# Regrouping the recurrent step of a bidirectional RWKV-7 layer by TensorE tile size

## The chip, the cores and the metric

The kernel runs on one core of one Trainium2 chip, as one program. The metric is the device time of one execution in microseconds (us). Before the change the median of three runs is 1908.73 us (1905.5 to 1909.22).

## The reference

Two layers work on 1024 latent tokens and 256 context tokens of width 1024, in float32. The first layer holds 12 RWKV-7 heads of width 64 and a Fourier mixing; the second is a multi-scale retention. What concerns us is the state recurrence of the first layer, which runs in both directions (`d == 1` reversed), context before latents:

```python
def step(s, inp):
    r_t, w_t, k_t, v_t, kk_t, b_t = inp
    sa = jnp.einsum('bhij,bhj->bhi', s, kk_t)
    s = s * w_t[:, :, None, :] - sa[..., None] * b_t[:, :, None, :] + v_t[..., None] * k_t[:, :, None, :]
    return s, jnp.einsum('bhij,bhj->bhi', s, r_t)
```

The outputs of both directions are added, each head is normalised over its 64 values, multiplied by a gate, and projected.

## The kernel before, in words

**The chunks.** The recurrence is computed in chunks of 64 tokens: 1280 tokens make 20 chunks. A *step* handles one chunk of four heads (two head pairs `q`) in both directions `d`; the index `x` = 2`d`+`q` and the half `h` name the eight units of a step. Three groups of four heads make 60 steps, `s` = 0 to 59; `c` is the chunk within its group. Inside a chunk the sequential dependence becomes a triangular 64x64 system for each unit. Its matrix comes out of the *scores* (product of the chunk's keys `bkp` with its queries `arr`, then a mask), and the step multiplies by the inverse of it.

**The inverse.** It is made in 32x32 blocks. GpSimd inverts the two diagonal blocks of all units of eight steps at once: 8 steps x 8 units x 2 blocks are its 128 partitions. `inv` does this in 31 rows, each a multiply (L1183) and an add (L1185) on a tile `z` with the triangle `tl`. The triangles reach it through DRAM: `diag` (L1142) writes the scores of each step to `dn`, and `fetch_tl` (L1170) reads `tl` back. The result goes to DRAM as `dz` (L1189), and `bring` (L1201) spreads it, in four transfers for four steps, over a tile `zs`. The off-diagonal block is made on TensorE in two small products, `offd1` (L1218, whose right side `x1p` VectorE transposes at L1206) and `offd2` (L1229).

**The step.** On TensorE a step issues: `ws` (L1423), scores of a later step (L1135), `up` (L1451), `offd1` of the next step, four transposes `pt` (`tok`, L1161), the state's increment `pst` into `ws` (L1488), `offd2`, the part of the output that comes from the state (L1513), the part from this chunk (L1516), and the other direction's scores (L1135). ScalarE copies `ws` to `wt` (L1428, two copies) and `up` to `vu` (L1456). VectorE adds state and increment into a tile `tmp` (L1492), multiplies by the decay `pc` into `vu` (L1496) and into the next state (L1497), and masks the scores (L1138).

**What sets the order.** The order is that of the program text, engine by engine; each engine and each DMA queue runs its own list in order. Scores run `L` = `LL` steps ahead of the step. The 31 rows of an inversion are dealt out over four *slots* of each step (`RW`), and `rows_until(s)` issues the rest, and `bring`, when step `s` needs them. `norm` is the head normalisation of 256 tokens, a generator that `stage` advances once in a step: TensorE centres (`pcen`, L1243), VectorE reduces (`rv`, L1252 and L1253), GpSimd takes the power -1/2 and multiplies (L1254 and L1258, the *pair* in what follows), TensorE transposes (`pgn`, L1262). All transfers named here but `dz` are issued by SyncE (SP), whose list they share with the loads of `arr`, `bkp` and `vu`.

Of the kernel before, what the change touches and what calls it, by code (L numbers as in the profile page):

```python
# [1039 lines left out]
def phaseB(g):  # L1040
# [83 lines left out]
    def scores(s, ds=(0, 1)):  # L1124

        if not 0 <= s < NS:
            return
        if s % 8 == 0 and ds[0] == 0:
            DN[s // 8] = dr.tile([steps(s // 8), 8, 64, 64], F32, tag="dn", name=f"dn{s // 8}")
        sc = SC[s] = SCR[s % (L + 1)]  # L1130
        ps = ps2.tile([128, 2, 512], F32, tag="psc", name=f"psc{s}_{ds[0]}")
        for d in ds:
            for x in (2 * d, 2 * d + 1):
                for h in range(2):
                    mm(ps[:, h, 128 * x : 128 * x + 128], lhsT=BK[s][H[h], x, :], rhs=AR[s][H[h], x, :], start=True, stop=True, tile_position=(64 * h, 0))  # L1135
# [1072 lines left out]
```

## Time and profile before

| | us |
|---|---|
| median of three runs | 1908.73 |
| profiled execution | 1913.79 |
| its span | 1912.0 |
| projections and gates, to 657.50 | 657.50 |
| start of the recurrence, to 695.52 | 38.02 |
| 60 steps, 695.52 to 1166.85 | 471.33 |
| second layer and projections, to the end | 745.15 |

The numbers of the next sections come from the one profiled execution, whose times count from the start of its span. In the 60 steps TensorE is busy for 389.50 us, GpSimd for 284.96, ScalarE for 259.61 and VectorE for 253.94, at a granted TensorE clock of 0.91 of full speed. Before them the share is 580.32 of 657.50 us for TensorE, and behind them 723.65 of 745.15 us. A line's row gives its start, its duration, the engine, the line, out<-in, the tile's form, and in brackets how long the engine was idle ahead of it and what ended that. A group of matrix products is shown as one row; its duration includes a modelled end, so the distance between two starts is the better measure of a group.

### The profile page before, as it was taken

How to read it: one execution, taken by the hardware profiler on the slowest of the kernel's cores; microseconds unless marked ns; L12 is line 12 of the kernel's file. 1: busy time of each engine (PE TensorE's matmuls, PEld its weight loads, DVE VectorE, ACT ScalarE, POOL GpSimd, SP SyncE). 2: the span in 40 equal slices, each digit the busy share in tenths (PEclk: the TensorE clock that was granted, in tenths of full speed). 3: DMA queues.
4: the chain of work that ended last, by engine and by line, in shares of the span. 5: the costliest groups of instructions: out<-in, count | busy, mean ns of one | idle time of the engine just before them, and what ended most of it. 6: DMA issues, size and time to landing. Idle time of an engine off the chain costs nothing. (4 is left out here: it accounts for less than half of the span.)

```text
span 1912.0 us, 37942 instructions
## 1 busy us (share of the span) xinstructions
PE 1708.9 (89%) x15490; PEld 1438.3 (75%) x15490; DVE 1009.5 (53%) x1580; ACT 715.4 (37%) x1598; POOL 773.9 (40%) x894
## 2 busy tenths in 40 slices
PE   6999997879887766887888788999999999999998
PEld 4777776667765655776777676779889898898877
DVE  6532689888985144655565444553352533523643
ACT  5322544535431123555556565343221122212231
POOL 4331443343452717656686821122442414414310
PEclk9999999899998978998899888999999999999999
DMA  9571365446559365777777774442111101101162
GB/s 316 172 239 55 86 169 146 136 122 187 136 147 279 104 163 154 202 194 181 191 191 192 193 201 129 134 139 87 39 50 34 56 23 46 58 30 56 50 204 99
DMA packets 340529, 257.54 MB, mean 135 GB/s; under 512 B 109004, under 2 KB 291780, under 8 KB 340100
## 3 DMA queue, kind: packets, MB, share of 16 engines
q1 hardware_dynamic: 325796, 221.96, 41.7%
q10 hardware_dynamic: 10512, 18.62, 3.3%
q0 software_dynamic: 4048, 14.55, 2.1%
q8 instruction: 122, 2.00, 0.4%
q14 instruction: 51, 0.42, 0.1%
HBM read 175.20 MB, written 79.88 MB: 133 GB/s over the span
## 5 line engine op out<-in xcount | busy, mean ns | idle before, releaser
L1183 POOL TENSOR_TENSOR tp<-z,tl 128x31 f32<-128x31 f32 (+19 forms) x248 | 130.8, 527 | 135.2 <-DMA tl<-dn 116.9
L548 PE MATMUL pgm<-hh,wh 128*128 128x512 f32 (+1 forms) x624 | 170.4, 383 | 0.0
L548 PE MATMUL pgm<-hl,wh 128*128 128x512 f32 (+1 forms) x624 | 160.9, 367 | 0.0
L548 PE MATMUL pgm<-hh,wl 128*128 128x512 f32 (+1 forms) x624 | 159.6, 365 | 0.0
L526 POOL TENSOR_TENSOR wl<-wr,wh 128x512 fp32r<-128x512 f32 x60 | 86.6, 1447 | 179.6 <-ACT wh L524 179.6
L1185 POOL TENSOR_TENSOR z<-z,tp 128x31 f32<-128x31 f32 (+19 forms) x248 | 139.7, 563 | 19.4
L1135 PE MATMUL psc<-arr,bkp 64*128 64x128 f32 x960 | 87.0, 312 | 52.9 <-issue 23.3
L548 PEld LDWEIGHTS pgm<-hl,wh 128*128 128x128 f32 x624 | 107.2, 196 | 20.5 <-POOL hl L484 1.0
L548 PEld LDWEIGHTS pgm<-hh,wl 128*128 128x128 f32 x624 | 106.6, 194 | 19.3
L548 PEld LDWEIGHTS pgm<-hh,wh 128*128 128x128 f32 x624 | 104.3, 197 | 20.8 <-issue 6.2
L1135 PEld LDWEIGHTS psc<-arr,bkp 64*128 64x128 f32 x960 | 67.7, 204 | 66.0 <-issue 36.9
L1862 PE MATMUL pv<-wv,hh 128*128 128x256 f32 x640 | 117.2, 285 | 0.0
L1138 DVE TENSOR_TENSOR scr<-psc,mask 128x512 f32<-128x512 f32 x120 | 80.4, 687 | 61.3 <-PE psc L1135 61.3
L571 DVE SCALAR_TENSOR_TENSOR m<-pgm,dv,m 128x255 f32<-128x255 f32 (+2 forms) x108 | 105.1, 987 | 10.5 <-ACT m L561 7.7
L1492 DVE TENSOR_TENSOR tmp<-ws,state 128x256 f32<-128x256 f32 x54 | 22.9, 424 | 152.6 <-PE ws L1488 75.2
L1862 PEld LDWEIGHTS pv<-wv,hh 128*128 128x128 f32 x640 | 99.6, 192 | 0.1
L1601 PE MATMUL pow_eo<-w_eo,yhw_eo 128*128 128x512 f32 x320 | 90.2, 403 | 0.5 <-ACT w_eo L1567 0.4
L1862 PE MATMUL pv<-wv,hl 128*128 128x256 f32 x320 | 90.6, 283 | 0.0
L1428 ACT COPY wt<-ws 64x256 f32<-64x256 f32 x120 | 43.9, 366 | 88.9 <-PE ws L1423 87.4
L835 POOL TENSOR_TENSOR ar<-m,Pp 128x640 f32<-128x640 f32 (+2 forms) x30 | 36.5, 1226 | 98.6 <-ACT Pp L827 93.9
L1601 PE MATMUL pow_oo<-w_oo,yhw_oo 128*128 128x512 f32 x256 | 72.3, 397 | 0.5 <-DVE w_oo L1568 0.4
L1601 PEld LDWEIGHTS pow_eo<-w_eo,yhw_eo 128*128 128x128 f32 x320 | 60.7, 191 | 16.0 <-ACT w_eo L1567 1.1
(337 smaller groups left out, 4179.7 us busy)
## 6 DMA issues: line engine op xcount, KB each, us to landing
aw<-ada_w SPq DMA_DIRECT2D x16, 1024.0 KB, 10.1
wr<-w_ev SPq DMA_DIRECT2D x60, 256.0 KB, 3.8
scr_AR<-ar SPq DMA_DIRECT2D x24, 640.0 KB, 3.7
scr_BK<-bk SPq DMA_DIRECT2D x24, 640.0 KB, 4.8
arr<-scr_AR SPq DMA_DIRECT2D x60, 256.0 KB, 3.7
bkp<-scr_BK SPq DMA_DIRECT2D x60, 256.0 KB, 4.3
br<-scr_BK ACTq DMA_DIRECT2D x60, 256.0 KB, 4.3
x<-xin SPq DMA_DIRECT2D x20, 512.0 KB, 4.9
```

The lines of the kernel that those rows point to most:

```text
L526: nc.gpsimd.tensor_tensor(out=wl, in0=wr, in1=wh.bitcast(F32), op=ALU.subtract)
L548: g.nc.tensor.matmul(ps[:, b, :n], lhsT=st[:, k % 4, :], rhs=mv[:, k, c0 : c0 + n], start=(k == 0 and i == 0), stop=(k == 7 and i == 2))
L571: nc.vector.scalar_tensor_tensor(out=o, in0=i, scalar=g.muc[:, q, ft : ft + 1], in1=o, op0=ALU.mult, op1=ALU.add)
L835: nc.gpsimd.tensor_tensor(out=ar[:, cs, 64:128], in0=ch(proc(self.r, d, lo, n)), in1=Pp[:, cs, 1:65], op=ALU.mult)
L1135: mm(ps[:, h, 128 * x : 128 * x + 128], lhsT=BK[s][H[h], x, :], rhs=AR[s][H[h], x, :], start=True, stop=True, tile_position=(64 * h, 0))
L1138: tt(out=sc[:, 2 * d : 2 * d + 2], in0=src, in1=K["mask2"][:, d].unsqueeze(1).unsqueeze(1).broadcast_to([128, 2, 2, 128]), op=ALU.mult)
L1183: eng.tensor_tensor(out=tv, in0=ZZ[:, 0:k, s : s + 1].broadcast_to([U, k, n]), in1=TL[:, s : s + 1, s + 1 : 32].broadcast_to([U, k, n]), o ...
L1185: eng.tensor_tensor(out=zo, in0=zo, in1=tv, op=ALU.add)
L1428: nc.scalar.copy(WT2[H[h], h].rearrange("p x v -> p (x v)"), WS[H[h], 0:256])
L1492: tt(out=tmp, in0=inc, in1=STS[s % 2], op=ALU.add)
L1601: self.g.nc.tensor.matmul(ps[:, 512 * b : 512 * b + 512], lhsT=st[:, k, :], rhs=mv[:, 512 * b : 512 * b + 512], start=(k == 0 and i == 0), ...
L1862: mm(ps[:, 256 * e : 256 * e + 256], lhsT=st[:, k, c0 : c0 + 128], rhs=mv[:, k, :], start=(k == 0 and i == 0), stop=(k == 7 and i == 2))
```

## The change

- The TensorE work of a step is put in another order, by the size of the tile that a product uses. `scores` now computes both directions of one step at once, as 16 products on 64x64 tiles. `offd1`, the state's part of the output, `up` and the scores stand in a row; then `pst`, the chunk's part of the output and `offd2`; then `tok`.
- `up` works on 64x64 tiles with one `wt` of 128x256, written by one ScalarE copy (L1431) in place of two.
- `offd1` no longer reads `x1p`. GpSimd makes the transposed upper diagonal blocks itself: after an inversion it copies half of `z`, transposed, into the buffer `tl` (L1179), and writes that to DRAM as `dx` (L1180). `bring` adds four transfers for four steps (L1189), which put the transposed blocks into the score tiles `scr`. The two VectorE transposes of a step go.
- The sum of increment and state stays in PSUM (L1462), so that the multiplications by `pc` (L1464, L1465) read PSUM.
- Scores run 18 steps ahead in place of 17, five rows of an inversion are dealt to a step in place of six, `stage` moves to the end of a step, and PSUM is dealt out anew.

```diff
-LL = 17
+LL = 18
-RW = (2,2,1,1)
+RW = (2,1,1,1)
...
+    PSC = ps2.tile([128, 2, 512], F32, name="psc")
...
+    def scores(s):
+        for x in range(4):
+            for h in range(2):
+                for m in range(2):
+                    mm(PSC[H[m], h, 128 * x : 128 * x + 128], lhsT=BK[s][H[h], x, H[m]], rhs=AR[s][H[h], x, :], start=True, stop=True, tile_position=(64 * h, 64 * m))
+    def masked(s):
...
-                    mm(ps[:, h, 128 * x : 128 * x + 128], lhsT=BK[s][H[h], x, :], rhs=AR[s][H[h], x, :], start=True, stop=True, tile_position=(64 * h, 0))
...
         eng.dma_start(DZ, ZZ)
+        DX = dr.tile([U // 2, 32, 32], F32, tag="dx", name=f"dx{m}")
+        eng.tensor_copy(out=TL[: U // 2].rearrange("p t s -> p s t"), in_=ZZ[: U // 2])
+        eng.dma_start(DX, TL[: U // 2])
...
+        for c in range(4):
+            nc.sync.dma_start(SC[4 * q + c][0:32, :, :, 0:32].rearrange("t x h s -> t (x h) s"), DX[32 * i + 8 * c : 32 * i + 8 * c + 8].rearrange("u t s -> t u s"))
...
-                nc.vector.transpose(out=X1P[s % 2][0:32, h], in_=inverse_of(s)[64 * h : 64 * h + 32, :, 0:32])
...
-                mm(st.py[r0 : r0 + 32, 32 * x : 32 * x + 32], lhsT=sc[:, x, h, 32:64], rhs=X1[:, h, x, :], start=True, stop=True, tile_position=(0, r0))
+                mm(py[H[h], 32 * x : 32 * x + 32], lhsT=sc[0:64, x, h, 0:64], rhs=sc[0:64, x, h, 0:32], start=True, stop=True, tile_position=(0, 64 * h))
...
+        rows_until(s + 1)
...
+        slot(0)
+        pre(s)
+        offd1(s + 1)
+        offd1_out(s + 1)
...
+                mm(UP[H[h], 64 * x : 64 * x + 64], lhsT=z[H[h], x], rhs=WT1[H[h], x], start=True, stop=True, tile_position=(64 * h, 64 * h))
+        ahead = ns <= min(s + L, NS - 1)
+        if ahead:
+            scores(ns)
+        slot(1)
+        arow(s + 1)
...
+            if c:
+                tt(out=inc, in0=inc, in1=STS[s % 2], op=ALU.add)
...
+            tt(out=STS[1 - s % 2], in0=inc, in1=pc.broadcast_to([128, 4, 64]), op=ALU.mult)
+        if ahead:
+            scored()
+        fetch(s)
+        slot(2)
...
+        offd2(s + 1)
+        tok(s + 1)
+        offd2_out(s + 1)
...
+        stage(s)
...
         slot(3)
```

On GpSimd, around the end of an inversion in the middle of the stage (`z_7293` is the tile of one inversion and `z_8214` of the next; `rv`, `cg` are a normalisation's), stood:

```order
L1185 TENSOR_TENSOR z_7293<-z_7293,tp_7294 128x31
L1189 DMA dz_7884<-z_7293 128x1024
L1254 TENSOR_TENSOR rv_768_7793<-rv_768_7793,mhalf 128x8
L1258 TENSOR_TENSOR cg_768_7782<-cg_768_7782,rv_768_7793 128x512
L1178 MEMSET z_8214 128x1024
L1179 MEMSET z_8214 128x32
L1183 TENSOR_TENSOR tp_8215<-z_8214,tl_8066 128x31
L1185 TENSOR_TENSOR z_8214<-z_8214,tp_8215 128x31
```

and now, around the end of the inversion `z_6578`:

```order
L1173 TENSOR_TENSOR z_6578<-z_6578,tp_6579 128x31
L1177 DMA dz_7281<-z_6578 128x1024
L1179 COPY tl_6404<-z_6578 64x32x32
L1180 DMA dx_7283<-tl_6404 64x1024
L1166 MEMSET z_7506 128x1024
L1167 MEMSET z_7506 128x32
L1171 TENSOR_TENSOR tp_7507<-z_7506,tl_7330 128x31
L1173 TENSOR_TENSOR z_7506<-z_7506,tp_7507 128x31
```

A pair stood directly behind `dz`; now a copy and the transfer of `dx` stand there, and the next inversion's rows follow without it. The first pair now stands behind twelve instructions (six rows) of that inversion:

```order
L1173 TENSOR_TENSOR z_7506<-z_7506,tp_7507 128x5x27
L1171 TENSOR_TENSOR tp_7507<-z_7506,tl_7330 128x156
L1173 TENSOR_TENSOR z_7506<-z_7506,tp_7507 128x6x26
L1249 TENSOR_TENSOR rv_512_7550<-rv_512_7550,mhalf 128x8
L1253 TENSOR_TENSOR cg_512_7539<-cg_512_7539,rv_512_7550 128x512
L1171 TENSOR_TENSOR tp_7507<-z_7506,tl_7330 128x175
```

The other pair of the eight steps stood behind 16 instructions (eight rows) of the inversion; now it stands 40 instructions behind the first one, so that both are inside the rows. On SyncE's list, the place where the inverses of four steps (`zs`) and the next triangles (`tl`) are fetched read:

```order
L1142 DMA dn_6271<-scr_5225 64x8x64
L1201 DMA zs_5231<-dz_6977 32x16x32 x4
L1096 DMA arr_5214<-scr_AR 128x512
L1098 DMA bkp_4605<-scr_BK 128x512
L1142 DMA dn_6271<-scr_5226 64x8x64
L1106 DMA vu_7098<-scr_VT 64x1024
L1170 DMA tl_7142<-dn_6271 64x32x32 x2
L1096 DMA arr_5215<-scr_AR 128x512
L1098 DMA bkp_4606<-scr_BK 128x512
```

and reads now:

```order
L1130 DMA dn_7275<-scr_5287 64x8x64
L1086 DMA arr_5274<-scr_AR 128x512
L1088 DMA bkp_4607<-scr_BK 128x512
L1189 DMA scr_5290<-dx_7283 32x8x32
L1189 DMA scr_5291<-dx_7283 32x8x32
L1189 DMA scr_5292<-dx_7283 32x8x32
L1189 DMA scr_4620<-dx_7283 32x8x32
L1194 DMA zs_5293<-dz_7281 32x16x32 x4
L1158 DMA tl_7330<-dn_6467 64x32x32 x2
L1130 DMA dn_7275<-scr_5288 64x8x64
L1086 DMA arr_5275<-scr_AR 128x512
L1088 DMA bkp_4608<-scr_BK 128x512
```

Four transfers from `dx` come ahead of `zs`, and `tl` follows `zs` directly. On TensorE one step, from `ws` to the next `ws`, was:

```order
L1423 MATMUL ws<-vu_6875,scr_5227 64x64 x8
L1135 MATMUL psc_0_7054<-arr_5212,bkp_4606 128x128 x8
L1451 MATMUL up<-wt_5264,zs_4627 64x64 x8
L1218 MATMUL py_7078<-x1p_5252,scr_5228 32x32 x8
L1161 MATMUL pt_7090<-ident,br_6988 128x128 x4
L1488 MATMUL ws<-vu_6875,bt_6979 64x64 x8
L1229 MATMUL py_7078<-zs_4627,y2p_5253 32x32 x8
L1513 MATMUL pyo_7125<-arr_5215,state_5262 64x64 x8
L1516 MATMUL pyo_7125<-scr_5227,vu_6875 64x64 x8
L1423 MATMUL ws<-vu_6875,scr_5228 64x64 x8
L1135 MATMUL psc_0_7158<-arr_5213,bkp_4607 128x128 x4
```

and is now:

```order
L1430 MATMUL ws<-vu_6813,scr_5287 64x64 x8
L1204 MATMUL up<-scr_5288 64x32 x8
L1441 MATMUL pyo_6997<-arr_5274,state_5321 64x64 x8
L1444 MATMUL up<-wt,zs_4628 64x64 x8
L1119 MATMUL psc<-arr_4619,bkp_4607 64x128 x16
L1459 MATMUL ws<-vu_6813,bt_7073 64x64 x8
L1472 MATMUL pyo_6997<-scr_5287,vu_6813 64x64 x8
L1219 MATMUL up<-zs_4628,y2p_5310 64x32 x8
L1149 MATMUL pt_7185<-ident,br_7082 128x128 x4
L1430 MATMUL ws<-vu_7036,scr_5288 64x64 x8
```

The four groups from L1204 to L1119 now stand in a row, with `offd1` second in the step, ahead of `up`.

## Rows read from the trace of the kernel before

**Rows 1.** Busy time by stretch: PE, PEld, DVE, ACT, POOL, clock, DMA share, GB/s.

```profile
695.52:1166.85 471.33, 389.50 (x8011) 329.29 (x8012) 253.94 (x560) 259.61 (x730) 284.96 (x481) 0.91 0.72 185
876.88:936.74 59.86, 51.59 (x1060) 44.10 (x1060) 36.39 (x77) 31.46 (x89) 41.21 (x70) 0.90 0.74 190
```

**Rows 2.** List of waits of the 60 steps: total us, times, longest us.

```profile
POOL tp L1183 <- DMA tl<-dn: 113.5, 6, 40.9
PE pgn L1262 <- POOL cg L1258: 28.2, 5, 7.5
```

**Rows 3.** Timeline of GpSimd between two inversions and into the second.

```profile
877.18 0.64 POOL L1189 DMA_DIRECT2D dz<-z  x1 [0.30 <-POOL z L1185]
877.85 1.66 POOL L1254 TENSOR_TENSOR rv<-rv,mhalf 128x8 f32<-128x8 f32 x1
879.59 1.04 POOL L1258 TENSOR_TENSOR cg<-cg,rv 128x512 f32<-128x512 f32 x1
880.57 0.95 POOL L1178 MEMSET z<- 128x1024 f32 x1
...
895.14 0.24 POOL L1183 TENSOR_TENSOR tp<-z,tl 128x31 f32<-128x31 f32 x1 [13.41 <-DMA tl<-dn]
...
900.08 0.49 POOL L1185 TENSOR_TENSOR z<-z,tp 128x156 f32<-128x156 f32 x1
...
902.99 1.83 POOL L1254 TENSOR_TENSOR rv<-rv,mhalf 128x8 f32<-128x8 f32 x1
```

**Rows 4.** Timeline of SyncE's queue in the same stretch.

```profile
880.18 1.91 SPq L1201 DMA_DIRECT2D zs<-dz  x4
...
887.65 1.78 SPq L1170 DMA_DIRECT2D tl<-dn  x2
```

**Rows 5.** Timeline of GpSimd: last rows of two inversions, first of the last.

```profile
815.49 0.27 POOL L1185 TENSOR_TENSOR z<-z,tp 128x31 f32<-128x31 f32 x1
...
1056.87 0.27 POOL L1185 TENSOR_TENSOR z<-z,tp 128x31 f32<-128x31 f32 x1
...
1062.96 0.23 POOL L1183 TENSOR_TENSOR tp<-z,tl 64x31 f32<-64x31 f32 x1
```

**Rows 6.** Timeline of TensorE in step 13.

```profile
806.66 0.69 PE L1423 MATMUL ws<-vu,scr 128*64 128x64 f32 x16
...
808.89 0.45 PE L1218 MATMUL py<-x1p,scr 128*32 128x32 f32 x16
809.26 0.66 PE L1161 MATMUL pt<-ident,br 128*128 128x128 f32 x4
...
810.84 0.68 PE L1513 MATMUL pyo<-arr,state 64*64 64x64 f32 x16
811.45 0.69 PE L1516 MATMUL pyo<-scr,vu 128*64 128x64 f32 x16
812.06 0.72 PE L1135 MATMUL psc<-arr,bkp 64*128 64x128 f32 x8
812.71 0.28 PE L1423 MATMUL ws<-vu,scr 128*64 128x64 f32 x2
```

**Rows 7.** Timeline of TensorE: a group of 128x32 tiles.

```profile
1082.26 0.65 PE L298 MATMUL padb<-scr,SL 128*32 128x128 f32 x16
```

**Rows 8.** Timeline of TensorE: a wait, and the start of step 25.

```profile
880.68 1.11 PE L1262 MATMUL pgn<-ident,cg 128*128 128x128 f32 x4 [7.50 <-POOL cg L1258]
...
898.33 0.69 PE L1423 MATMUL ws<-vu,scr 128*64 128x64 f32 x16
```

**Rows 9.** Timeline of VectorE in step 25.

```profile
901.28 0.50 DVE L1253 TENSOR_SCALAR rv<-rv 128x8 f32<-128x8 f32 x1
```

**Rows 10.** Timeline of GpSimd in the second layer.

```profile
1329.29 2.40 POOL L1843 TENSOR_TENSOR wq<-wrq,wq 128x1024 fp32r<-128x1024 f32 x1 [12.98 <-ACT wq L1841]
```

**Rows 11.** Timeline of VectorE: the same operation twice.

```profile
806.26 0.71 DVE L1497 TENSOR_TENSOR state<-tmp,pc 128x256 f32<-128x256 f32 x1
...
884.31 0.42 DVE L1497 TENSOR_TENSOR state<-tmp,pc 128x256 f32<-128x256 f32 x1
```

More of the change, by code (lines that the diff above doesn't have):

```diff
@@ L22 @@
 EW = 3
-NP = 4
 NQ = 0
-DF = 0
 NB = 3
@@ L1410, in phaseB @@
     st.wait = WT[1:]
-    for s in range(-1, NS):
+    load_group(0)
+    for i in range(PR):
+        more(-1)
+        rows(RW[i % 4])
+    rows_until(0)
+    offd1(0)
+    offd1_out(0)
+    tok(0)
+    offd2(0)
+    offd2_out(0)
+    arow(0)
+    load_late(1)
+    for s in range(NS):
         gi, c = divmod(s, 20)
-        live = s >= 0
+        st.s = s
         if c == 16:
             load_group(gi + 1)
-        for b0 in {2: (256, 1024), 6: (512, 768)}.get(c, ()) if live else ():
+        for b0 in {2: (256, 1024), 6: (512, 768)}.get(c, ()):
@@ L1429, in phaseB @@
[L1429 to L1438 removed]
+        ar, sc, vu, z = AR[s], SC[s], VU[s // 2][:, s % 2], inverse_of(s)
+        pc = PCS[gi].rearrange("p d q c -> p (d q) c")[:, :, c : c + 1]
+        rows_until(s + 1)
+        for x in range(4):
+            for h in range(2):
+                mm(WS[H[h], 64 * x : 64 * x + 64], lhsT=sc[:, x, h, 0:64], rhs=vu[:, x, h], start=True, stop=True, tile_position=(0, 64 * h))
@@ L1439, in phaseB @@
+        nc.scalar.copy(WT1.rearrange("p x v -> p (x v)"), WS[:, 0:256])
         slot(0)
         pre(s)
-        n0 = ns
-        more(s, (2 if s in CU else 1) if live else PQ)
-        early = TK == 1 and live and ns == n0
-        if early:
-            tok(s + 1)
-        if JW:
-            late_sum(s)
-        if live:
+        offd1(s + 1)
+        offd1_out(s + 1)
+        if c % 2 == 0:
+            PY = pw.tile([128, 4, 2, 64], F32, tag="py", name=f"pyo{s}", bufs=2)
+        for x in range(4 if c else 0):
+            for h in range(2):
+                mm(PY[H[h], x, c % 2], lhsT=STS[s % 2][H[h], x], rhs=ar[H[h], x, 64:128], start=x == 0, stop=False, tile_position=(64 * h, 64 * h))
@@ L1463, in phaseB @@
-        if not DF:
-            while dgs:
-                diag(*dgs.pop(0))
+                tt(out=VU[(s + 1) // 2][0:64, (s + 1) % 2, :, h], in0=inc[H[h]], in1=pc[H[h]].broadcast_to([64, 4, 64]), op=ALU.mult)
+            tt(out=STS[1 - s % 2], in0=inc, in1=pc.broadcast_to([128, 4, 64]), op=ALU.mult)
+        if ahead:
+            scored()
+        fetch(s)
+        slot(2)
+        for x in range(4):
+            for h in range(2):
+                mm(PY[H[h], x, c % 2], lhsT=vu[:, x, h], rhs=sc[:, x, h, 64:128], start=c == 0 and x == 0, stop=x == 3, tile_position=(0, 64 * h))
@@ L1466, in phaseB @@
+        if c % 2 == 1:
+            for d in range(2):
+                (off, n, lo), = pieces(d, 64 * (c - 1), 128)
+                b0 = lo // 256 * 256
+                yv = Y[gi, b0][:, :, lo - b0 : lo - b0 + 128]
+                if d == 1:
+                    yv = yv[:, :, ::-1]
+                tt(out=yv, in0=PY[:, 2 * d : 2 * d + 2].rearrange("p q c t -> p q (c t)"), in1=yv, op=ALU.add)
+        offd2(s + 1)
+        tok(s + 1)
+        offd2_out(s + 1)
         if s == YS:
@@ L1531, in phaseB @@
+        if s in CU:
+            more(s)
+        for b0 in {3: (0,), 15: (512, 768), 19: (256, 1024)}.get(c, ()):
+            nms.append(norm(gi, b0))
         slot(3)
@@ L1751, with __init__ @@
 class Gens:
-    def __init__(self, three, one):
-        self.p, self.n = (three, three, three, one), 0
+    def __init__(self, one, two):
+        self.p, self.n = (one, one, two, two), 0
     def tile(self, shape, dtype, tag, name):
```

212 lines of the change are left out of this document (57 added, 155 removed).

## The prediction

> **What bounds the kernel now.** I read the windows first. TensorE is busy for 389.50 of the 471.33 us of the 60 steps, the only stretch that the change touches in earnest; 82 us are not TensorE's [rows 1]. The list of waits says who holds it up: GpSimd waits six times, 113.5 us in all, for its triangles (`tl`), and TensorE 28.2 us in five waits for the normalisation's product, which GpSimd makes [rows 2]. So I followed a loop through the timelines. An inversion ends at 877.18 less 0.30, at 876.88. `dz` is issued at 877.18 and SyncE, which has waited for it, issues `zs` at 880.18: landing takes 3.0 us. `tl` is issued at 887.65, behind four other kinds of transfer; GpSimd's next row starts at 895.14, 7.5 us later, after 13.41 us idle [rows 3, 4]. So an inversion starts 18.3 us behind the end of the one before, and lasts to 936.74 (the edge of the window in [rows 1]), 41.6 us. From the end of inversion 2 (815.76) to that of inversion 6 (1057.14) are four such loops in 241.4 us, 60.3 us for eight steps or 7.5 us a step [rows 5].
>
> A step that nobody holds up is shorter: step 13 goes from 806.66 to 812.71, 6.05 us [rows 6]. The loop through GpSimd, DRAM and SyncE, not TensorE, sets the pace of the middle of the stage. TensorE catches up and stops once in eight steps, at `pgn` [rows 8].
>
> **TensorE's part.** A group of sixteen records with 32 columns starts 0.37 us before the next one, a group with 64 columns 0.61 (810.84 to 811.45) [rows 6]. The extra 32 columns cost 0.24, so 64 cost 0.48 and each group bears 0.13 that doesn't depend on columns. I put that down to the change of tile shape, since nearly every group before differs from its neighbour. After the change there are four changes of shape in a step in place of ten: six times 0.13, 0.8 us off a step, to some 5.25. Over 60 steps that is 48 us, if TensorE set the end.
>
> The scores of one direction took 0.65 for 4 products of 128 columns, two at a time [rows 6], both 1.3; four at a time on 64x64 tiles they need the same streaming once, and one change less. That four tiles run at once is shown by 128x32 tiles only: 16 records of 128 columns in 0.65 [rows 7]. If 64x64 tiles ran by twos the scores would cost 0.9 us more; I take four.
>
> The Trainium skill, "TensorEngine Tiling (Array Packing)", Gotcha 1, says that different row tiles cannot use the same PSUM bank at the same time. By it `up` and `offd1`, now on row tiles that share a bank, would run singly. The row speaks against it: the state's product has 64x64 tiles in both halves of the rows, in one bank, and takes the 0.61 of the group behind it [rows 6]. By the rule a step would be 0.7 us longer, by the row nothing; I go by the row.
>
> **The loop, step by step.** Let E be the end of an inversion's rows.
>
> 1. E + 0.3: `dz`, issue 0.67 [rows 3]. Now the transposing copy, with no row of its own. Bounds: a clear of 128x1024 takes 0.95 [rows 3], a multiply of 128x1024 with two inputs 2.40 [rows 10]. The copy has one input and 64 partitions; I take 1.2, nearest to the clear. `dx` is then issued at about E + 2.3 and lands 3.0 later as `dz` did: E + 5.3 (5.0 to 6.5). Before, `zs` could go at E + 3.3.
> 2. SyncE: four issues of `dx` to `scr`, then four of `zs`, at 1.91 for four [rows 4]: `tl` is issued at E + 9.1, where it was at E + 10.8, because `arr`, `bkp`, `dn` and `vu` no longer stand between. With the same 7.5 the next inversion starts at E + 16.6, 1.7 earlier than before. The landing could vary by 1 us either way.
> 3. The rows. Before, one pair of power and multiply stood inside them; the other stood right behind `dz` and lay in the time in which GpSimd waited for `tl`. Now both are inside. A pair takes 2.75 (877.85 to 880.57 and the end of its multiply, 879.59 + 1.04) [rows 3], so the rows take 41.6 + 2.75 = 44.35. Without any new wait the loop is 16.6 + 44.35 = 61 us, hardly other than 60.3.
> 4. The new wait. The first pair needs `rv` from VectorE, made in the second step behind the delivery of `dx`. Six rows end 5.43 us behind the start (900.57) [rows 3], at E + 22. When is `rv` there? `offd1` of the next step needs the blocks of `dx`: SyncE issues at E + 5.3, landing takes 2 to 3, so TensorE resumes at E + 7.8, after a long stop. The rest of that step, whose `offd2` waits for `zs` until about E + 11.5, ends at E + 12 to 14. Behind a stop TensorE is slow: the four transposes behind the wait took 1.11 us, those of step 13 0.66 [rows 6, 8], at a granted clock of 0.90 over the loop [rows 1]. So the first step, 5.25 when fast, takes 5.5 to 6, and the second starts at E + 18 to 20. Before, `rv` came 3.45 us behind a step's start (898.33 to 901.78) [rows 8, 9]. Now `stage` stands last, so VectorE reaches it behind the sum, three products, two masks and the outputs: 8 to 8.8 us behind the start. `rv` is there at E + 26 to 28.8. GpSimd would wait for 4 to 6.8 us; queued behind the waiting power are 25 rows, the whole rest of the inversion, and behind them TensorE's next eight steps. The wait could also be nothing, if the steps catch up sooner.
> 5. Rows can get cheaper. The state's multiplication took 0.71 with GpSimd at work and 0.42 while it waited [rows 11]; two engines hinder each other there, and after the change that operation reads PSUM. I take 1 us a loop, bounds 0 and 3. The Trainium skill, "SBUF — State Buffer", in "SBUF: two separate sides", calls the port pair that VectorE and GpSimd share an exclusive lock: a VectorE operation with two SBUF inputs and a GpSimd operation that reads SBUF wait for each other. The trace agrees, at 0.71 against 0.42; by the rule the whole 3 us would come off.
>
> Sum: 16.6 + 44.35 + 4 (the wait's lower end, nearer to no wait) − 1 = 64 us, 3.3 to 3.6 more than before. The eight steps themselves, 42 us, fit in the loop, so the 0.8 us that each saves becomes a longer stop of TensorE. Four loops: +13.
>
> **The two ends.** The start: copy and `dx` delay the clears that follow inversion 0 by 2 us, and eight transfers in place of four stand ahead of the second `tl` (1.9): +3 (0 to 5). The end: before, the last `tl` went out as soon as its buffer was free and the last inversion began at 1062.96, 5.8 us behind the sixth [rows 5]. Now it stands behind `bring`, so it begins 16.6 behind and ends later by 11 and the wait. But in between TensorE was the bound, with eight steps that save 0.8 each, and the last four save again, −10. I take 0 (−6 to +8). Edits at nothing: VectorE's transposes and ScalarE's second copy, which both lay beside TensorE; the second layer, whose PSUM tiles rotate over four as before.
>
> Sum: +13 + 3 + 0 = +16 on the profiled execution's 1913.79 us, which lies 5.1 above the median of the runs. So the runs should show 1924.7; I say 1924.
>
> **Rivals.**
>
> *Rows cheaper, and no wait.* If `rv` is in time (VectorE's list is shorter by the transposes) and the port is worth 3 us, a loop is 61 − 2.5 = 58.5, 1.8 less, four make −7; with a start of +2 and an end of −5 the sum is −10: 1899. For it: 0.71 against 0.42. Against: `stage` is at the step's end, and TensorE stands before `dx`.
>
> *In between.* A wait of 0 to 2 us gives a loop of 60 to 62 and a sum of −3 to +4: about 1908.
>
> *Longer than I say.* The copy at 2.4 and a wait of 6.8, with TensorE at half its clock throughout the first step, give a loop of 67: 4 times 6.7 is 27, with start and end 35: 1943. It decides from a `rv` later than E + 28.
>
> *TensorE sets the end.* All 48 us come off, to 1861. Against it: the waits of [rows 2], none of which the regrouping takes away.
>
> *The regrouping does not do what it says*: scores on 64x64 tiles run by twos, or the 0.13 us is not from the shape. A step stays at 6.05 or more, and `rv` comes two steps' worth later, 1 to 2 us a loop on top: 1930. The page's rule on banks would end there too.
>
> **How the numbers follow.** My forecast has 0.44, with 1912 to 1934 as its own range (wait from 2 to 6 us); no wait 0.28; in between 0.11; longer 0.11; TensorE as the bound 0.03; no regrouping 0.03. A measurement of this kernel tells some 0.2%, 3.8 us, from no change. Faster: 0.28 + 0.03 and a little of the middle, 0.32. Same: the rest of the middle and the lower edge of the forecast, 0.13. Slower: 0.55. To hold the time eight times in ten the range reaches from the case without a wait to the long one: 1895 to 1942.
>
> **What would show it.** In the profile after: GpSimd's wait for `rv` at the first pair, 4 us and more, once in eight steps; next inversion's first row 16 to 17 us behind the last one's end; ends of inversions 64 us apart; fast steps of 5.2 to 5.3 us; TensorE stopped for 15 us and more ahead of `offd1` with the cause `dx`. I am wrong if the ends lie 59 us apart or less, if the power finds `rv` ready, or if TensorE has no long stop.

## The result, and the profile after

The changed kernel takes 1968.37 us (median of 4 runs, 1965.25 to 1970.91) beside 1908.31 for the one before: 1.0317 times as long (95% interval 1.0298 to 1.0335). The direction was forecast, the size was not: +60 measured, +16 forecast, and the time lies outside the range. The profiled execution took 1970.91 us.

| us | before | after | |
|---|---|---|---|
| ahead of the 60 steps | 695.5 | 693.1 | −2.4 |
| step 0 to the end of inversion 2 | 120.2 | 126.9 | +6.7 |
| four loops, end of inversion 2 to end of 6 | 241.4 | 275.9 | +34.5 |
| end of inversion 6 to the last step's end | 109.7 | 125.5 | +15.8 |
| second layer and projections | 745.1 | 747.7 | +2.6 |

The 57 us more lie in the 60 steps, as the windows show, against the two rows of [rows 1]. First the whole stretch, then one loop (columns as there):

```profile
693.08:1221.39 528.31, 385.26 (x8732) 335.69 (x8732) 196.39 (x441) 233.56 (x665) 292.22 (x495) 0.87 0.67 169
891.87:959.67 67.80, 49.43 (x1208) 44.03 (x1208) 29.18 (x62) 31.07 (x88) 42.23 (x72) 0.88 0.72 181
```

TensorE, VectorE and ScalarE are all busy for less time than before (VectorE by 57.6 us), and the stretch is longer. So the loss is waiting. From the list of waits of these steps (total us, times, longest us), to be read against [rows 2]:

```profile
POOL tp L1171 <- DMA tl<-dn: 130.6, 7, 52.3
POOL rv L1249 <- DVE rv L1248: 80.0, 7, 33.1
PE up L1204 <- DMA scr<-dx: 49.3, 6, 10.2
PE pgn L1257 <- POOL cg L1253: 27.5, 5, 15.1
```

The waits for `dx` are new. The kernel before had waits for `rv` too, three of them:

```profile
POOL rv L1254 <- DVE rv L1253: 33.5, 3, 28.7
```

All three of those lie behind the sixth inversion, and 33.2 of the 33.5 us behind the last one; none lies in a loop. After the change the longest of the 80.0 us, 33.1, lies behind the last inversion too and holds up little. New are one wait of 7.5 to 9.8 in each of the loops, and two of 14.0 in all in the last inversion.

Now one loop, from the end of an inversion at E = 891.87. GpSimd's timeline, against [rows 3]:

```profile
892.17 0.64 POOL L1177 DMA_DIRECT2D dz<-z  x1 [0.30 <-POOL z L1173]
892.81 1.93 POOL L1179 COPY tl<-z 64x1024 f32<-64x1024 f32 x1
895.04 0.54 POOL L1180 DMA_DIRECT2D dx<-tl  x1 [0.30 <-POOL tl L1179]
...
909.34 0.24 POOL L1171 TENSOR_TENSOR tp<-z,tl 128x31 f32<-128x31 f32 x1 [12.59 <-DMA tl<-dn]
...
922.13 1.67 POOL L1249 TENSOR_TENSOR rv<-rv,mhalf 128x8 f32<-128x8 f32 x1 [7.55 <-DVE rv L1248]
923.88 1.04 POOL L1253 TENSOR_TENSOR cg<-cg,rv 128x512 f32<-128x512 f32 x1
```

SyncE's queue in the same loop, against [rows 4]:

```profile
897.92 1.80 SPq L1189 DMA_DIRECT2D scr<-dx  x4
899.81 3.04 SPq L1194 DMA_DIRECT2D zs<-dz  x4
902.96 1.89 SPq L1158 DMA_DIRECT2D tl<-dn  x2
```

TensorE, the restart behind `dx` and the start of the next two steps, against [rows 8]:

```profile
899.73 0.92 PE L1204 MATMUL up<-scr 64*64 64x32 f32 x13 [9.86 <-DMA scr<-dx]
...
906.69 0.69 PE L1430 MATMUL ws<-vu,scr 128*64 128x64 f32 x16 [0.54 <-issue]
...
913.12 0.69 PE L1430 MATMUL ws<-vu,scr 128*64 128x64 f32 x16
```

VectorE's last operation on `rv`, against [rows 9]:

```profile
921.88 0.17 DVE L1248 TENSOR_SCALAR rv<-rv 128x8 f32<-128x8 f32 x1
```

Read in order of time: the copy takes 1.93, `dx` is issued at E + 3.2 and taken up by SyncE at E + 6.05; `tl` goes out at E + 11.1, and the rows start at E + 17.5. TensorE has restarted at E + 7.9, and its second step starts at E + 21.25. The windows of these two steps (from the restart, and from the next `ws`):

```profile
899.73:906.69 6.96, 6.42 (x133) 6.00 (x133) 1.80 (x5) 2.46 (x8) 0.00 (x0) 0.71 0.70 104
906.69:913.12 6.43, 6.29 (x157) 5.75 (x157) 4.50 (x10) 3.70 (x13) 3.08 (x10) 1.00 0.98 199
```

The first runs at a granted clock of 0.71, partly at the lower level of 1.2 GHz, behind a stop of TensorE of 9.86 us; the second at the full level. In the step that starts there `stage` is last on VectorE's list, so `rv` is ready 8.9 us behind the step's start, at E + 30.2. GpSimd has stood at the power since E + 22.7, with 25 rows behind it. The inversion lasts 50.3 us: 37.3 of rows, two pairs of 2.75, 7.55 of waiting. Before it was 41.6. The start behind E has become 0.8 shorter (18.3 before), the inversion 8.7 longer.

The ends of inversions 2 and 6, and the first row of the last, against [rows 5]:

```profile
819.73 0.27 POOL L1173 TENSOR_TENSOR z<-z,tp 128x31 f32<-128x31 f32 x1
...
1095.65 0.27 POOL L1173 TENSOR_TENSOR z<-z,tp 128x31 f32<-128x31 f32 x1
...
1110.85 0.23 POOL L1171 TENSOR_TENSOR tp<-z,tl 64x31 f32<-64x31 f32 x1 [10.06 <-DMA tl<-dn]
```

The loops are 71.9, 67.8, 68.3 and 68.0 us, mean 69.0. The last inversion starts 14.9 behind the sixth (5.8 before) and lasts until 1167.67, 56.8 us (42.1 before), with its 14.0 of waiting.

Last, step 12, which has no long stop in it, against [rows 6]:

```profile
805.80 0.69 PE L1430 MATMUL ws<-vu,scr 128*64 128x64 f32 x16 [0.48 <-issue]
806.42 0.59 PE L1204 MATMUL up<-scr 64*64 64x32 f32 x13
806.90 0.66 PE L1441 MATMUL pyo<-arr,state 64*64 64x64 f32 x15
807.70 0.62 PE L1444 MATMUL up<-wt,zs 64*64 64x64 f32 x13
808.21 1.04 PE L1119 MATMUL psc<-arr,bkp 64*64 64x128 f32 x30
809.18 0.73 PE L1459 MATMUL ws<-vu,bt 128*64 128x64 f32 x16
809.70 0.68 PE L1472 MATMUL pyo<-scr,vu 128*64 128x64 f32 x16
810.17 0.66 PE L1219 MATMUL up<-zs,y2p 128*64 128x32 f32 x16
810.75 0.66 PE L1149 MATMUL pt<-ident,br 128*128 128x128 f32 x4
811.92 0.69 PE L1430 MATMUL ws<-vu,scr 128*64 128x64 f32 x16 [0.52 <-DVE state L1465]
```

It takes 6.12 us from `ws` to `ws`, where 5.25 was forecast and 6.05 stood before. The scores take 0.97 for all four tiles (808.21 to 809.18), so the tiles do run four at a time. Two gaps eat the gain. `ws` waits 0.52 for VectorE's state. And `up` starts 0.80 behind the state's product, a group of 0.6: it writes the PSUM tile `UP`, of which ScalarE still reads another part, the result of `offd1`:

```profile
807.12 0.53 ACT L1211 COPY y2p<-up 32x128 f32<-32x128 f32 x2 [0.18 <-PE up L1204]
```

### The profile page after: what moved, and what is told of

Its sections match the earlier page's. It is cut to its first block, busy times and chain, and to the rows that moved or that the text cites. A ratio compares the mean times of both kernels' runs of the same rounds, so it can differ in the third digit from the quotient of the medians.

```text
span 1969.1 us, 39642 instructions
## 1 busy us (share of the span) xinstructions
PE 1703.9 (87%) x16450; PEld 1441.8 (73%) x16450; DVE 945.6 (48%) x1457; ACT 691.1 (35%) x1538; POOL 782.0 (40%) x906
## 5 line engine op out<-in xcount | busy, mean ns | idle before, releaser
L1171 POOL TENSOR_TENSOR tp<-z,tl 128x31 f32<-128x31 f32 (+19 forms) x248 | 126.9, 512 | 153.2 <-DMA tl<-dn 135.5
L1462 DVE TENSOR_TENSOR ws<-ws,state 128x256 f32<-128x256 f32 x54 | 23.4, 433 | 256.3 <-PE ws L1459 226.5
L1173 POOL TENSOR_TENSOR z<-z,tp 128x31 f32<-128x31 f32 (+19 forms) x248 | 134.2, 541 | 19.4
L1119 PE MATMUL psc<-arr,bkp 64*64 64x128 f32 x1920 | 81.0, 307 | 41.5 <-DVE scr L1125 28.6
L1119 PEld LDWEIGHTS psc<-arr,bkp 64*64 64x64 f32 x1920 | 64.6, 153 | 48.2 <-DVE scr L1125 32.7
L1204 PE MATMUL up<-scr 64*64 64x32 f32 x960 | 43.4, 233 | 51.7 <-DMA scr<-dx 49.3
L1204 PEld LDWEIGHTS up<-scr 64*64 64x64 f32 x960 | 36.8, 148 | 56.8 <-issue 36.5
L1150 ACT COPY bt<-pt 128x512 f32<-128x512 f32 x60 | 35.2, 586 | 112.2 <-PE pt L1149 112.2
```

Source lines behind the costliest of these rows:

```text
L1119: mm(PSC[H[m], h, 128 * x : 128 * x + 128], lhsT=BK[s][H[h], x, H[m]], rhs=AR[s][H[h], x, :], start=True, stop=True, tile_position=(64 * h ...
L1171: eng.tensor_tensor(out=tv, in0=ZZ[:, 0:k, s : s + 1].broadcast_to([U, k, n]), in1=TL[:, s : s + 1, s + 1 : 32].broadcast_to([U, k, n]), o ...
L1173: eng.tensor_tensor(out=zo, in0=zo, in1=tv, op=ALU.add)
L1204: mm(py[H[h], 32 * x : 32 * x + 32], lhsT=sc[0:64, x, h, 0:64], rhs=sc[0:64, x, h, 0:32], start=True, stop=True, tile_position=(0, 64 * h))
```

## The experiments

Theory W: the pair's place. `stage` at the step's end makes `rv` late, the pair stands six rows into the inversion, and GpSimd's list waits. Rivals: F, the fetch (`dx` and `zs` ahead of `tl`) sets the loop; and the sum in PSUM, or shared PSUM tiles, holds the steps up. In the headings stand the median and its ratio to the kernel before with its 95% interval; a loop is the mean of the four from inversion 2 to 6.

**1. `rv` one step earlier: 1930.83 us, 1.0128 [1.0092, 1.0164].** The generator pauses ahead of the power, no longer ahead of the reduction.

```diff
-        yield
...
+        yield
         nc.gpsimd.tensor_tensor(out=rv, in0=rv, in1=K["mhalf"].broadcast_to([128, 8]), op=ALU.pow)
```

> The changed kernel with one line moved: the normalisation's reduce and scaling (rv) are issued one step earlier, the power and multiply stay where they are. Theory W (GpSimd's wait for rv, 7.5 us once in eight steps, paces the loop): rv comes some 6 us earlier, the wait falls to 0 to 2 us, ends of inversions lie 61 to 63 us apart instead of 68, and the kernel gets 25 to 40 us faster (1928 to 1943). Rival F (the delivery of dx and the fetch of tl over SyncE pace the loop): no more than 5 us. Rival P (the step itself, with new waits for shared PSUM tiles, sets the end): no more than 5 us.

```profile
898.42 1.67 POOL L1249 TENSOR_TENSOR rv<-rv,mhalf 128x8 f32<-128x8 f32 x1 [2.10 <-DVE rv L1247]
```

The wait is 2.10 in place of 7.55, the loop 63.3 in place of 69.0, and by the medians 37.5 of the 60 us are back. In the profiled executions the 60 steps take 498.2 in place of 528.3, which is 30 of the 57 us; what lies ahead of them, which the edit does not touch, differs by another 9.8 between these two executions. W is shown to carry more than half of the loss. Nothing else of the change was touched.

**2. `stage` ahead of the sum: 1945.04, 1.0207 [1.0173, 1.0242].**

```diff
+        stage(s)
         if c < 19:
...
-        stage(s)
```

> The changed kernel with stage back in the middle of the step, ahead of the state's increment, as it stood before the change. rv is made some 5 us earlier, but the pair also stands one slot (one row) earlier in GpSimd's list. Theory W: the wait for rv falls from 7.5 to 3 to 4 us, the loop from 68 to 64, the kernel by 15 to 25 us. Rivals F and P: within 5 us of the changed kernel.

```profile
906.19 1.67 POOL L1249 TENSOR_TENSOR rv<-rv,mhalf 128x8 f32<-128x8 f32 x1 [2.81 <-DVE rv L1248]
```

The wait is 2.81, the loop 64.4, and 23 us are back: the same wait is shortened in another way.

**3. Rows dealt out faster: 2000.4, 1.0477 [1.0441, 1.0512].**

```diff
-RW = (2,1,1,1)
+RW = (3,3,2,2)
```

> The changed kernel with one line of constants other: ten rows of an inversion dealt to a step in place of five, so that the first pair stands behind 22 rows instead of 6 and the second one behind dz, as before the change. Theory W (GpSimd's wait for rv paces the loop): no wait is left and one pair leaves the rows; the loop falls from 68 us to 57 to 60, the kernel by 40 to 55 us, to 1913 to 1928. Rival F (delivery and fetch): the loop stays at 66 and more, the kernel within 8 us. Rival P (the step): within 5 us.

Meant to move the pair out of the rows, it moved the wait instead. The timeline of GpSimd:

```profile
909.63 1.66 POOL L1249 TENSOR_TENSOR rv<-rv,mhalf 128x8 f32<-128x8 f32 x1 [19.22 <-DVE rv L1248]
...
920.38 0.24 POOL L1171 TENSOR_TENSOR tp<-z,tl 128x31 f32<-128x31 f32 x1 [6.85 <-DMA tl<-dn]
```

An inversion, with one pair in it, takes 40.0 to 40.5 us. But the other pair now stands between `dz` and the next rows and waits 19.22 for `rv`. The step that makes this `rv` is itself held up: TensorE stands in it for 3.92 us (7.30 in the next loop) for `bkp`, which SyncE issues behind `dx` and `zs`. The inversions start 24.5 to 33.7 behind E, and the loop is 71.2. This is a miss; the cause is the same, a list in order with a late input, at another place.

**4. `tl` ahead of `bring`: 1977.91, 1.0378 [1.0348, 1.0407].**

```diff
+        if back and back[0][0] <= s // 4 and new and not ivs and s > 0:
+            begin()
```

> The changed kernel with the fetch of the next triangles (tl) issued ahead of the bring of dx and dz on SyncE. The next inversion starts some 5 us earlier, at 12.5 us behind the last one's end instead of 17.4; dx arrives about 2 us later. Theory W: GpSimd only waits longer for rv (14 us instead of 7.5), the loop stays at 68 or grows to 70, the kernel is 0 to 12 us slower. Rival F: the loop falls by 5 us, the kernel by 20 to 25 us. Rival P: no change.

```profile
902.67 0.23 POOL L1171 TENSOR_TENSOR tp<-z,tl 128x31 f32<-128x31 f32 x1 [7.59 <-DMA tl<-dn]
...
925.68 1.67 POOL L1249 TENSOR_TENSOR rv<-rv,mhalf 128x8 f32<-128x8 f32 x1 [16.61 <-DMA br<-scr_BK]
```

In the loops the rows start 12.4 to 14.8 behind E in place of 17.2 to 18.9, and all of it, and more, goes into a longer wait at the power: 16.61. (The row names a transfer as what ended it; `rv` was ready at 925.60, 0.08 ahead of the power.) The loop is 72.5. F falls as far as it concerns the fetch of `tl`: while `rv` is late, an earlier start is worth nothing. It does not fall for `dx`: with `tl` ahead of it TensorE restarts 12.9 behind E in place of 7.9, `rv` comes at E + 35.4 in place of 30.2, and the loop grows by 3.5. The delivery of `dx` is the first part of the way to `rv`.

**5. The sum in SBUF again: 1977.8, 1.0385 [1.0349, 1.0421].**

```diff
+            tmp = sm.tile([128, 4, 64], F32, tag="tmp", name=f"tmp{s}", bufs=1)
...
-                tt(out=inc, in0=inc, in1=STS[s % 2], op=ALU.add)
+                tt(out=tmp, in0=inc, in1=STS[s % 2], op=ALU.add)
...
```

> The changed kernel with the sum of state and increment written to an SBUF tile again, as before the change. If the first product of a step waits for VectorE's last read of the sum in PSUM, an undisturbed step gets 0.4 us shorter (6.12 to 5.7); the two steps between dx and rv make the loop 1 us shorter, the tail of 12 steps gains 4 us: the kernel gets 5 to 12 us faster (theory W). Rival P (steps set the end): 0.4 us times 60, 24 us faster. If the VectorE operations with two SBUF inputs slow GpSimd's rows again by 1 to 2 us a loop, 0 to 8 us slower instead.

A miss: no time comes back, so the sum in PSUM is no part of the loss. Without it `ws` waits 0.15 to 0.20 in place of 0.52, but a step takes 6.08 as ever, since the multiplication into `vu` with both inputs in SBUF takes 1.1 to 1.25 in place of 0.85. The rows take 38.1 to 38.3 in place of 37.1, and the loop 70.1.

**6. PSUM tiles apart: 1983.99, 1.0403 [1.0373, 1.0432].** The off-diagonal results go to a tile of their own, the increment to the free half of `UP`.

```diff
-        py = UP[:, 256:384]
+        st.py = gtile(f"py{s}")
+        py = st.py[:, 0:128]
...
-                pst = WS[:, 256 + 64 * x : 320 + 64 * x]
+                pst = UP[:, 256 + 64 * x : 320 + 64 * x]
```

> The changed kernel with the results of the two off-diagonal products in a PSUM tile of their own and the state's increment in the tile of up: the first product of a step no longer waits for VectorE's reading of the sum (0.52 us in a step), nor up for the copy of the off-diagonal result (0.25). If these two waits took the 0.8 us that fewer changes of tile shape give, an undisturbed step falls from 6.12 to 5.3 to 5.5 us. If the chain ws, wt, up, vu, pst, sum, vu through ScalarE and VectorE sets the step instead, it stays at 5.8 or more. The kernel: theory W 8 to 20 us faster (the two steps ahead of rv and the last twelve), rival P 40 us faster, rival F under 5.

TensorE in step 21:

```profile
867.06 0.69 PE L1431 MATMUL ws<-vu,scr 128*64 128x64 f32 x16
...
868.65 0.57 PE L1445 MATMUL up<-wt,zs 64*64 64x64 f32 x13
...
872.24 0.33 PE L1431 MATMUL ws<-vu,scr 128*64 128x64 f32 x2
```

This step takes 5.18 us, and undisturbed steps take 5.18 to 5.57. So the regrouping does save time in a step, and the shared tiles hid it. It is not quite the 0.8 us of the forecast, because step 13 of the kernel before had a wait in it, in the rows left out of [rows 6]:

```profile
807.63 0.72 PE L1135 MATMUL psc<-arr,bkp 64*128 64x128 f32 x8 [0.28 <-DVE scr L1138]
```

Without that wait its products took 5.77, so that 0.2 to 0.6 us of the saving belong to the regrouping. The loop stays at 68.7 (the wait for `rv` is 8.60), so the faster steps buy nothing. The kernel is slower than the changed one because its end is (137.9 behind inversion 6, in place of 125.5): inversion 7 takes 72.5 us, of which 29.7 are waits for `rv`. Normalisation and off-diagonal results now share two buffers; that this is the reason was not tested.

**7. Test 1, rows dealt faster, `bring` later: 1956.33, 1.0246 [1.0212, 1.028].** The last value of `WT` puts `bring` off on SyncE's list, so that `tl` is fetched ahead of it.

```diff
-WT = (3,6,3)
+WT = (3,6,16)
...
-RW = (2,1,1,1)
+RW = (3,3,2,2)
```

> The changed kernel with rv a step earlier, ten rows dealt to a step, and bring delayed in SyncE's list so that tl is fetched ahead of it. Theory W taken to its end: no wait for rv, the next inversion 12 to 14 us behind the last one's end, the loop 52 to 54 us, and TensorE's eight steps of 6.3 us become the bound: 1870 to 1895, faster than both kernels. Rival F: SyncE's list now blocks at bring or tl at another place, loop 60 and more, 1915 and more.

This is a miss. `tl`, early in SyncE's list, stands there behind triangles (`dn`) of steps that are not done yet, and `bring` stands behind `tl`: TensorE stops for 9.2 to 11.3 us for a `dx` that has landed in DRAM long ago. The loop is 63.4, no shorter than in test 1.

**8. The same on the kernel before: 1940.76, 1.017 [1.0135, 1.0206].** Same two lines, and `LL = 18`; by the program text a buffer of late modulation weights is then used again too soon, so that what follows the recurrence isn't the reference's.

> The kernel before with scores 18 steps ahead, ten rows dealt to a step and bring delayed, so that tl is fetched ahead of zs; its TensorE work and its inverses are those of before. If the loop through GpSimd, DRAM and SyncE paces the kernel before as well, the next inversion starts 7 to 9 us behind the last one's end instead of 18.3, the loop falls from 60.3 to 50 to 53 us, and the kernel to 1860 to 1885. If TensorE's own work paces it, 1900 and more.

A miss as well: the loops are 57.6, 64.4, 66.9 and 68.2. The rows of before were not dealt too slowly; the early fetch does harm on SyncE's list there too, where transfers of `dn` wait for VectorE for 88 us in 20 waits.

**9 and 10. The pair off GpSimd, after: 1958.75, 1.0256 [1.0208, 1.0305]; before: 1910.1, 0.9994 [0.9961, 1.0026].** A square root on ScalarE and a reciprocal on VectorE replace the power; the multiply goes to VectorE too.

```diff
-N2 = 1
+N2 = 0
...
-        yield
...
-        nc.gpsimd.tensor_tensor(out=rv, in0=rv, in1=K["mhalf"].broadcast_to([128, 8]), op=ALU.pow)
+        nc.scalar.activation(rv, rv, AF.Sqrt)
+        yield
+        nc.vector.reciprocal(rv, rv)
```

> The changed kernel with the pair taken off GpSimd: ScalarE takes the square root behind rv, VectorE the reciprocal and the multiply a step later. Nothing but the inversions is left on GpSimd in the loop. If its pair (the wait for rv of 7.5 us, twice 2.75 us of its own, and TensorE's wait for its result) is what the change lost, the loop falls from 68 us to 54 to 57 (17.4 from end to start and 36.8 for the rows, or eight steps and their stop), the last inversion gets 13 us shorter, and the kernel comes to 1885 to 1910. If the delivery of dx through SyncE and the stop of TensorE (rival F) pace it, the loop stays at 62 and more: 1935 and more.

> The kernel before with the same edit, the pair taken off GpSimd. One pair (2.75 us) leaves the rows of each loop and TensorE's 28 us of waiting for it go, most of which lay in the time of delivery anyway: the loop falls from 60.3 to 56 to 58 us, the kernel by 10 to 20 us, to 1887 to 1897. Against the run of the changed kernel with this edit it says what the rest of the change is worth: if that one is faster, the regrouping itself gains and only its schedule of the pair loses.

After, no power waits inside the rows (inversions of 38.2 to 41.8; the two longest hold waits of 3.2 and 1.8 ahead of a clear of `vu`), and the loop falls to 61.8, about where rival F had put it. It doesn't fall further, since the next start moves to 19.7 to 25.8 behind E:

```profile
903.23 0.23 POOL L1171 TENSOR_TENSOR tp<-z,tl 128x31 f32<-128x31 f32 x1 [16.49 <-DMA tl<-dn]
```

The eight steps of triangles must exist before they are inverted, and each step with a square root takes longer, as `up` waits 1.6 to 2.0 us for ScalarE. In the kernel before, the loop goes from 60.3 to 59.2 and the time stays the same, where 10 to 20 us less was expected.

**11. Test 1, and the late modulation ahead of the step's end: 1929.13, 1.0098 [1.0069, 1.0128].** In the late steps of the changed kernel TensorE does the modulation's second product last, and waits for ScalarE: 

```profile
1126.85 0.65 PE L287 MATMUL padb<-scr,SL 128*32 128x128 f32 x16
...
1128.30 0.38 PE L328 MATMUL padb<-sel,adap 128*128 128x2 f32 x2 [0.81 <-ACT adap L289]
```

Thirteen such waits cost 9.3 us behind inversion 6 of the changed kernel.

```diff
             scores(ns)
+        late_sum(s)
         slot(1)
...
+        while ajobs:
+            late_ada.second(ajobs.pop(0))
         offd2(s + 1)
...
-        late_sum(s)
-        while ajobs:
-            late_ada.second(ajobs.pop(0))
```

> The changed kernel with rv a step earlier, and the late modulation sums of steps 44 to 59 taken from the step's end to where they stood before: the first product behind the scores, the second ahead of offd2. In the changed kernel the last steps take 7.3 us and 5.7 in the kernel before, with TensorE waiting for ScalarE's copy between the two products (0.8 us) and for vu (0.47). If that is a part of the loss of its own, a late step falls to 6.0 to 6.5 us and the kernel to 1910 to 1920, 12 to 20 us under the one with rv alone (1930.8). If the last steps are paced by something else, within 4 us of that one.

The shortest late steps go from 7.30 to 6.25, the end behind inversion 6 from 119.3 in test 1 to 107.9, the 60 steps from 498.2 to 488.8. The median fell only by 1.7 us; the part ahead of step 0, which the edit does not touch, was 12.6 longer here in the profiled execution. Shown in the stage, unclear in the total.

**12 and 13. Without `dx`: 1910.84, 1.0006 [0.9987, 1.0026], and 1904.53, 0.9983 [0.9959, 1.0006].** Test 11 with GpSimd's copy and `dx` taken out; VectorE transposes straight into the score tiles, and `offd1` stands behind `pst`. In test 12 the copy of `arr` stands ahead of `offd1`, so the off-diagonal blocks aren't the reference's; in test 13 it stands behind.

```diff
-        eng.tensor_copy(out=TL[: U // 2].rearrange("p t s -> p s t"), in_=ZZ[: U // 2])
-        eng.dma_start(DX, TL[: U // 2])
...
+                nc.vector.transpose(out=SC[s][0:32, :, h, 0:32], in_=inverse_of(s)[64 * h : 64 * h + 32, :, 0:32])
...
```

> As the kernel with rv early and the sums moved, and the delivery of the transposed inverses over DRAM undone: no copy and no dx on GpSimd, VectorE transposes as before the change, offd1 behind the state's increment. tl is fetched directly behind zs, and offd1 waits for zs alone: the next inversion starts 12 to 14 us behind the last one's end (17.4 with dx, 18.3 before), the wait for rv is 0 to 3 us, the loop 56 to 59 us. If the delivery of dx is a part of the loss of its own (rival F, as far as it holds), the kernel is 12 to 25 us faster than with dx, 1890 to 1905, and faster than the kernel before. If only rv and the sums counted, within 5 us of the one with dx.

> The regrouped step with rv a step early, the sums moved and VectorE transposes in place of dx, as in the run with vector transposes, with the copy of arr behind offd1 so that the products read what they should. The loop is 60 to 62 us and the kernel 1900 to 1912, level with the kernel before. If the copy's place matters (ScalarE's list), up to 8 us more.

GpSimd of test 13:

```profile
890.06 0.23 POOL L1171 TENSOR_TENSOR tp<-z,tl 128x31 f32<-128x31 f32 x1 [6.44 <-DMA tl<-dn]
...
899.83 1.66 POOL L1250 TENSOR_TENSOR rv<-rv,mhalf 128x8 f32<-128x8 f32 x1 [4.53 <-DVE rv L1248]
```

The rows start 14.0 behind E, the loop is 60.7 (before 60.3), and a step 5.71. Test 13 is 64 us faster than the changed kernel and 25 faster than test 11: that is what the delivery of `dx`, together with the early place of `offd1` that needs it, cost on top of the pair. Most of the regrouping is kept in it, and it is level with the kernel before.

**14. Test 13 with the pair off GpSimd: 1911.93, 1.0027 [1.001, 1.0043].**

> The same with the pair taken off GpSimd (ScalarE's square root, VectorE's reciprocal and multiply). If the regrouping is worth 0.2 to 0.8 us a step once GpSimd no longer holds it up, the loop falls to 52 to 56 us (14.4 from end to start and 37.5 of rows; eight steps of 6.0 to 6.5) and the kernel to 1875 to 1895, faster than both kernels. If the steps with their ScalarE and VectorE chain, or the delivery of zs, pace it, the loop stays at 58 to 62 and the kernel at 1900 to 1912, as the same edit did nothing for the kernel before.

The loop is 58.1, the shortest of all, but steps with a square root take 7.1 to 7.3. There is no gain.

**15. The kernel before with `stage` late and five rows a step: 1936.64, 1.0145 [1.0114, 1.0177].** The counter-test to 1: the pair gets the changed kernel's place by two constants (`NP2 = 3` puts `stage` behind the third slot), without any regrouping.

```diff
-NP2 = 0
+NP2 = 3
...
-RW = (2,2,1,1)
+RW = (2,1,1,1)
```

> The kernel before with two constants other: stage stands late in the step, and five rows are dealt to a step in place of six. GpSimd's list then has the changed kernel's order: the first pair 7 rows into the inversion, the second one inside the rows too. Nothing of the regrouping is in it. If the place of the pair is the main loss (theory W), the loop grows from 60.3 to 64 to 68 us with a wait for rv of 3 to 7 us, and the kernel to 1930 to 1950. If the loss needs dx or the regrouped step, it stays within 8 us of 1908.

```profile
811.54 0.27 POOL L1185 TENSOR_TENSOR z<-z,tp 128x31 f32<-128x31 f32 x1
...
913.55 1.66 POOL L1254 TENSOR_TENSOR rv<-rv,mhalf 128x8 f32<-128x8 f32 x1 [14.60 <-DVE rv L1253]
...
1083.33 0.28 POOL L1185 TENSOR_TENSOR z<-z,tp 128x31 f32<-128x31 f32 x1
```

The wait of 14.60 appears in the kernel before, the inversion takes 57 to 58 us, and the four loops 271.8, 67.9 each, like the changed kernel's. The parts are not the same: the rows start 8.3 behind E in place of 17.5 (SyncE issues `tl` ahead of `zs` here), and the wait is 7 us longer. What agrees is when the power can run, at E + 29.5 here and at E + 30.3 in the changed kernel, with 24 and 25 rows behind it. The pair's place by itself is enough for the loop of the changed kernel, and by test 1 most of the loop's growth needs it.

## Why the prediction was wrong, step by step

**Right, or nearly.** The loop through GpSimd as the bound; a wait for `rv` at the first pair of every loop, as the cause; `offd1` resuming at E + 7.8 (7.86); the first step's start at E + 12 to 14 (14.8) and the second's at 18 to 20 (21.25), a little early; `rv` 8 to 8.8 behind the step's start (8.9); four tiles at once (0.97 for the scores); rows about 1 us cheaper (37.1, before 38.0 and 38.8 without a pair), and not 3. Of its signs, TensorE's stop ahead of `offd1` came with the cause that it named, `dx`, but lasted 9.86 us and not 15 and more.

**The wait (step 4), the term that failed.** The forecast had it at 4 to 6.8 us and took 4, the lower end, as "nearer to no wait", for which its sum of the steps gave no reason. It was 7.55, beyond the range. `rv` came at E + 30.2 in place of 26 to 28.8, since small delays add: the restart to the next `ws` took 6.96 us, and the step behind it 6.43 in place of 5.5 to 6, so that the second step started at 21.25. With the measured terms the sum is 17.5 + 37.3 + 5.5 + 7.55 = 67.8, the loop as it was. The four loops came out 20 us longer than four times the forecast's 64: the waits, 32.9 in place of 16, make 16.9 of it, the starts 4.6, and the rows take 1.4 back. Tests 1 and 15 show that this is the mechanism, not only a story: 37.5 us off with most of the wait gone, 30 on with the pair's place alone.

**The delivery (steps 1 and 2).** 16.6 forecast, 17.5 measured: the copy, and `zs` issues of 3.04 in place of 1.91. `tl` left at E + 11.1, not 9.1, so landing was quicker than before. That the loop could be as long as 67 was there as a rival, with a chance of 0.11 and with its reasons (a slower copy, a later `rv`, TensorE slow behind its stop); it came out longer by 2.

**The end, "0 (−6 to +8)", the second term that failed.** Measured +15.8. The start of the last inversion was well put (9.1 later, 11 forecast), but "the wait" was 14.0 in two places there, not 4, and the −10 from steps that save 0.8 each wasn't to be had: late steps take 7.30 (5.69 before), held for the most part by the modulation's second product at the step's end, which the sum left out (6.25 with it elsewhere, test 11). Behind inversion 7 the stage is 8 us shorter (53.7, before 61.8); the inversion cost 24 (9.1 + 14.7).

**The start, +3 (0 to 5).** Measured +6.7, counted from step 0. All of it is there when the rows of inversion 1 start, 27.4 behind step 0 in place of 20.6. Which transfer made it was not tested.

**TensorE's step, 5.25.** Measured 6.1. For products alone the result was right (test 6: 5.18 to 5.57), though the step that it started from, 6.05, had 0.28 of waiting in it. Two waits through shared PSUM tiles were not priced: `up` behind the copy of `offd1`'s result, `ws` behind the state. Wrong in number, without weight for the time: loop 68.7 with the fast steps, 69.0 without.

**The rivals.** No wait and in between are refuted by 7.55. That TensorE sets the end is refuted by test 6. "The regrouping does not do what it says" had its step time right, 6.1, for a reason it didn't name, and the scores by twos are refuted.

**What stays open.** From the changed kernel to test 13 the medians give back 37.5 (`rv`), 1.7 (late modulation) and 24.6 us (`dx`), 64 in all. The first is 30.1 in the stage and the middle one 9.4, so the three parts are not cleanly apart. How much of the last is the missing copy, how much the shorter list of SyncE, and how much the later place of `offd1`, was not taken apart. No version beat the kernel before beyond its interval.

## What to carry to other kernels

An instruction that waits on an engine whose list runs in order holds up all that is queued behind it, whatever its own length: pairs of 2.75 us, moved to a place where their input is late, cost 30 us and more here. Start the producer one step earlier (test 1); starting the queue earlier or emptying it faster only moves the wait (tests 3 and 4). When a wait is worked out as a sum of delays, take the middle of its range at least: here every delay on the way to `rv` came out at or beyond the upper end of its range.

## What the runs showed of the hardware

- A 128x64 tile for 32 columns takes 0.58 a group (L1219, 810.17 to 810.75), where a 128x32 tile took 0.37 [rows 6]: the extra width is paid.
- Tiles of 64x64 in both halves of the rows wrote one bank side by side: `offd1` 0.48 and `up` 0.51 a group. The prediction weighed a rule there, from the Trainium skill, "TensorEngine Tiling (Array Packing)", Gotcha 1, that different row tiles cannot access the same PSUM bank simultaneously; as the prediction read it, these products would run singly. No row here shows that.
- Reading one part of a PSUM tile holds a write to another part of it in this program: 0.44 to 0.52 us a wait, and 0.5 to 0.9 us a step come back when the tiles are apart (test 6).
- VectorE's multiplication into `vu` with GpSimd at work: 0.85 with an input in PSUM, 1.1 to 1.25 with both in SBUF (test 5). The one into the state: 0.42 with an input in PSUM, 0.61 to 0.76 with both in SBUF (test 5), and 0.42 with both in SBUF while GpSimd waited [rows 11].
- The transposing copy of 64x1024 on GpSimd takes 1.93, twice the clear of 128x1024 [rows 3].
- In test 9 ScalarE loads a table once for its square roots, 1.28 us at 737.42:

```profile
737.42 1.28 ACT L1248 ACT_TABLE_LOAD   x1
```
